# A decoder layer with sparse experts: VectorE instead of GpSimd computes the remainders and the modulation in front of the first expert

## The chip, the cores and the metric

The kernel runs on 1 core of one Trainium2 chip. The metric is the device time of one execution in microseconds (us). The engines are TensorE (PE, with its weight loads as PEld), VectorE (DVE), ScalarE (ACT), GpSimd (POOL) and SyncE (SP), which issues most DMA transfers. Less is better.

## The reference

One layer on 512 tokens of width 1024, in fp32, with two sub-layers:

```
cond = silu(c)
sh_m, sc_m, gt_m, sh_f, sc_f, gt_f = split(cond @ w_ada + b_ada, 6)
h = rms_norm(x, g_pre_mix) * (1 + sc_m) + sh_m
q_a, k_a, v_a, q_b, k_b, v_b, f = h @ w_in
y_a = attention of 8 heads with a cumulative log-forget-gate bias
y_b = block-sparse attention of 8 heads with a relative-position bias
x = x + gt_m * rms_norm(concat(y_a, y_b) @ w_out, g_post_mix)
h = rms_norm(x, g_pre_ffn) * (1 + sc_f) + sh_f
y = sum over the 4 best of 32 experts: gate * (swiglu(h @ w_gate_up[e] + b) @ w_down[e] + b)
x = x + gt_f * rms_norm(y, g_post_ffn)
```

## The kernel before, in words

**Products in two parts.** TensorE multiplies in the type fp32r, which keeps fewer bits than fp32. Each fp32 operand is therefore split: ScalarE copies it into an fp32r tile (the upper part, `hi`), and a subtraction gives the remainder, `lo = raw - hi`, also in fp32r. A product is the sum of hi x hi, hi x lo and lo x hi. The function `split` (L279 to L282) does this for the weights of the first sub-layer; `lo_part` (L1101) does it for the expert weights.

**Opening (0 to about 61 us).** The modulation vectors are `cond @ w_ada`. They are not computed on TensorE as matrix products; instead the eight row blocks of a column slice are multiplied by one value per partition and added up, and TensorE then sums over the partitions with a column of ones. For the two vectors needed first, shift and scale of the mixing sub-layer (SH_M and SC_M), there are four slices (q = 0 to 3) of 256 columns. Of the eight blocks of a slice VectorE does 5 (SC_M) or 6 (SH_M) in `ada_macs` (L360 for the first, L362 for the others) and GpSimd the remaining 3 or 2 in `ada_pool` (L374, L376). `ada_sums` (L383 on) adds the two partial sums on TensorE (L389), finishes scale and shift on VectorE (L396 to L398), and then applies them to two channels k of the transposed x: ScalarE writes the upper part and the full value (L401), and the remainder (L403) is VectorE's for even k and GpSimd's for odd k. Meanwhile `v_split` splits the weights of V, block by block, with the remainder on GpSimd (`G_`), and `v_mm` (L426) multiplies.

**V and projections (61 to about 125 us).** The second V group follows, with the forget gates and the biases between. `mac_step` (L262, L264) computes the other four modulation vectors on VectorE, 512 columns at a time, in steps spread over this stage and the attention. `qk_split` splits the weights of a query or key projection of two heads (eight blocks of 128 columns, so 128x1024), `qk_proj` (L561 to L563) multiplies, `evac_a` and `evac_b` (L575, L584, L587) take the result out of PSUM.

**Attention (125 to about 345 us).** There is one turn per head h, and a turn issues the work of neighbouring heads: a projection, the second product of head h-1, the transposes of head h's weights (`stage_b`, L667 to L671), the scores of head h+1, then its softmax (L631 on VectorE, L634 on ScalarE) and `normalize` (L643, L647: four products of 128, 256, 384 and 512 columns on VectorE). Behind the normalization come the next `qk_split` or, from head 11 on, `wo_split` for the output weights, and two `mac_step`s. `mix_out` (L694 to L701) adds the two halves of a head pair and splits the result for the output product; its remainder (L701) is GpSimd's.

**Output product, norms and router (345 to about 405 us).** Row blocks of 128 tokens pass through `wo_mm`, `post_norm`, `norm_h` and the router (`route_a`, L1003 to L1010). In `norm_h` GpSimd keeps two products and sums of 128x1024 (L971, L972). The raising to a power in `rstd` (L227) is GpSimd's as well. The first weight tile of the first expert is split just before the last `route_a`, with the remainder on GpSimd (L1101).

**Experts (from about 405 us).** Expert 0's rows are gathered from HBM by an indirect DMA that GpSimd issues (L1177); the number of tokens per expert gives the order of the others (`order_rank`, `order`). Its result `perm` (L1426) releases the stream of the other experts' weights, 12 tiles of 1 MB each, that SyncE issues as slots come free. Their remainders are VectorE's already. Only the second and third tile of expert 0 are shared: columns 0 to 1407 (`LO_V`) on VectorE, 1408 to 2047 on GpSimd.

**What sets the order.** The program is written out by hand: each engine runs its instructions in the order in which the code issues them, and waits at the head of its queue for what the next one needs. A weight tile's slot comes free (`W.release`) when its readers are done, and this lets SyncE issue the next load.

Of the kernel before, what the change touches and what calls it, by code (L numbers as in the profile page):

```python
# [11 lines left out]
F32 = mybir.dt.float32  # L12
# [4 lines left out]
OP = mybir.AluOpType  # L17
# [4 lines left out]
RING2, RING3 = 3, 1  # L22
LO_V = 1408

# [72 lines left out]
def build(tc, io, dbg=None):  # L97
    nc = tc.nc
    with ExitStack() as ctx:
# [180 lines left out]
        def split(raw, hi, lo, lo_eng=None):  # L280
            nc.scalar.activation(hi, raw, AF.Copy)  # L281
            (lo_eng or nc.gpsimd).tensor_tensor(lo, raw, hi.bitcast(F32), op=OP.subtract)  # L282

# [12 lines left out]
        with ExitStack() as st:  # L296
# [51 lines left out]

            NPE = {SC_M: 3, SH_M: 2}
            aq, todo_q = {}, [(q, ch, k) for q in range(4) for ch in (SC_M, SH_M) for k in range(8 - NPE[ch])]  # L350

            def ada_macs(n):

                for _ in range(n):
                    q, ch, k = todo_q.pop(0)
                    if k == 0:
                        aq[q, ch] = xp.tile([128, 256], F32, name="accq", tag="accq", bufs=4)
                    a, w, c = aq[q, ch], W.tiles[ada_ids[ch, q]], cond[:, k:k + 1]
                    if k == 0:
                        nc.vector.tensor_scalar(a, w[:, k], c, None, op0=OP.mult)  # L360
                    else:
                        nc.vector.scalar_tensor_tensor(a, w[:, k], c, a, op0=OP.mult, op1=OP.add)  # L362
                    if k == 7 - NPE[ch]:
                        W.release(ada_ids[ch, q])

            def ada_pool(q, ch):
                if not NPE[ch]:
                    return
                w = W.tiles[ada_ids[ch, q]]
                X = [128, 256]  # L370
                ts = xp.tile([128, 2, 256], F32, name="accp", tag="accp", bufs=2)
                for k in range(8 - NPE[ch], 8):
                    t = ts[:, k % 2]
                    nc.gpsimd.tensor_tensor(t, w[:, k], cond[:, k:k + 1].to_broadcast(X), op=OP.mult)  # L374
                    if k > 8 - NPE[ch]:
                        nc.gpsimd.tensor_tensor(t, t, u, op=OP.add)  # L376
                    u = t
                aq[q, ch, 1] = u

            def ada_sums(q):  # L380

                ps = {}
                for ch in (SC_M, SH_M):  # L383
                    a = aq.pop((q, ch))
                    p = ps[ch] = ps1.tile([128, 2], F32, name="adaq", tag="adac", bufs=2)
                    parts = [aq.pop((q, ch, 1)), a] if NPE[ch] else [a]
                    for n, a in enumerate(parts):
                        for j in range(2):
                            nc.tensor.matmul(p[:, j:j + 1], a[:, 128 * j:128 * j + 128], ones,  # L389
                                             start=(n + j == 0), stop=(n + j == len(parts)))  # L390
                if AHEAD_Q[q]:
                    for ch in (SC_M, SH_M):
                        ada_pool(q + 1, ch)
                ada_macs(AHEAD_Q[q])
# [4 lines left out]
                for k in range(2 * q, 2 * q + 2):  # L399
                    for o in (hT[:, 0, k], xT[:, k]):  # L400
                        nc.scalar.activation(o, xT[:, k], AF.Identity, scale=a_m[:, k:k + 1], bias=modT[:, k:k + 1])  # L401
                    eng = nc.gpsimd if k % 2 else nc.vector
                    eng.tensor_tensor(hT[:, 1, k], xT[:, k], hT[:, 0, k].bitcast(F32), op=OP.subtract)  # L403

# [42 lines left out]

            G_ = nc.gpsimd
            per_q = len(todo_q) // 4
            AHEAD_Q = (3, 5, 6, 0)  # L450
            for ch in (SC_M, SH_M):
                ada_pool(0, ch)
            ada_macs(per_q)
# [7 lines left out]
            for q in range(4):  # L461
                if q < 3 and not AHEAD_Q[q]:
                    for ch in (SC_M, SH_M):
                        ada_pool(q + 1, ch)
                if q < 3:
# [84 lines left out]
        with ExitStack() as st:  # L550
# [135 lines left out]
            def mix_out(h):  # L686
# [9 lines left out]
                if s:  # L696
                    if p % 4 == 0:
                        MIX[g] = big.tile([128, 4, 2, 512], F32R, name="mix", tag="big")
                    m = MIX[g]
                    nc.scalar.activation(m[:, p % 4, 0], y, AF.Copy)  # L700
                    nc.gpsimd.tensor_tensor(m[:, p % 4, 1], y, m[:, p % 4, 0].bitcast(F32), op=OP.subtract)  # L701

# [185 lines left out]
        with ExitStack() as st:  # L888
# [218 lines left out]
            first[0] = hi_lo(first_raw(0))  # L1107
            lo_part(nc.gpsimd, first_raw(0), *first[0], 0, 2048)
            W.release(moe_ids[0, 0], False)
# [368 lines left out]
        order_rank()  # L1478
        for n in (1, 2):
            lo_part(nc.vector, first_raw(n), *first[n], 0, LO_V)  # L1480
            lo_part(nc.gpsimd, first_raw(n), *first[n], LO_V, 2048)
            W.release(moe_ids[0, n])
        nc.gpsimd.memset(xg[1], 0.0)
        blocks[0].w = first
        stage_x(blocks[0].tiles[0])
        for i, (p, n) in enumerate(seq[:-LAST]):
# [170 lines left out]
```

## Time and profile before

| | us |
|---|---|
| median of 3 runs | 1579.89 (1579.83 to 1581.43) |
| the profiled execution | 1584.43 |
| span of its profile | 1582.4 |
| busy in the span: TensorE, VectorE, ScalarE, GpSimd | 1431.8, 1004.6, 756.6, 367.8 |
| HBM read | 466.80 MB, 308 GB/s over the span |

The profile shows one execution. Its times are in us from the start of the span, and L12 is line 12 of the kernel. "Busy" is the time in which an engine executes instructions; a matrix product's end is modelled, so a busy TensorE need not be TensorE at its peak. The granted clock (PEclk) is 1.00 at full speed and 0.50 at half. A row names an engine, a line and an operation, then what is written, "<-" and what is read, with the shape; in brackets stands the idle time in front of it and what ended it.

### The profile page before, as it was taken

To read this page: it belongs to the slowest core of one execution; us is meant where nothing else is said; L and a number is where in the kernel's file an instruction comes from. 1 tells how busy PE (TensorE), PEld (TensorE's weight loads), DVE (VectorE), ACT (ScalarE), POOL (GpSimd) and SP (SyncE) were. 2 spreads that over 40 slices of the span, in tenths; PEclk is the share of its full clock that TensorE was granted. 3 is DMA by queue.
4 is the path that set the end of the run, shared out by engine and by line. 5 is a ranking of instruction groups with operands and counts; after the bars stand their busy time and mean duration, and the time that the engine had idled before them with its cause. 6 is when DMAs were issued, how large, how long until landed. Compare 5 with 4: busy or idle time off the path is not lost. (4 is left out here: it accounts for less than half of the span.)

```text
span 1582.4 us, 18315 instructions
## 1 busy us (share of the span) xinstructions
PE 1431.8 (90%) x6513; PEld 952.2 (60%) x6513; DVE 1004.6 (63%) x1287; ACT 756.6 (48%) x833; POOL 367.8 (23%) x268
## 2 busy tenths in 40 slices
PE   5898999989599999889999989998999999999992
PEld 4676777667475655647575646646565746666640
DVE  6785888876876664837374655727374748686532
ACT  5433565545364462726263553616263646475421
POOL 7542234434310212310010203310001203121002
PEclk8897999789699999999999999998999999999996
DMA  9652353364498999999699999999699999999994
GB/s 304 219 192 89 93 173 100 105 224 181 164 353 286 385 398 374 397 395 383 246 392 355 384 401 386 399 390 375 205 390 344 394 381 400 388 381 388 357 393 119
DMA packets 154757, 485.92 MB, mean 307 GB/s; under 512 B 13775, under 2 KB 35387, under 8 KB 154664
## 3 DMA queue, kind: packets, MB, share of 16 engines
q1 hardware_dynamic: 143807, 457.39, 76.8%
q0 software_dynamic: 10016, 24.59, 6.6%
q10 hardware_dynamic: 841, 2.75, 0.5%
q8 instruction: 52, 0.85, 0.2%
q14 instruction: 41, 0.34, 0.1%
HBM read 466.80 MB, written 19.85 MB: 308 GB/s over the span
## 5 line engine op out<-in xcount | busy, mean ns | idle before, releaser
L1101 DVE TENSOR_TENSOR mlo<-raw,mhi 128x2048 fp32r<-128x2048 f32 (+1 forms) x203 | 457.9, 2279 | 140.2 <-ACT mhi L1097 139.9
L1097 ACT ACTIVATE mhi<-raw 128x2048 fp32r<-128x2048 f32 x203 | 385.8, 1912 | 152.4 <-PE gu L1217 59.6
L1217 PE MATMUL gu<-mhi,xT 128*128 128x512 f32 x1152 | 402.0, 417 | 0.6 <-DVE xT L1193 0.6
L1322 POOL DMA_INDIRECT accd<-y,idx x33 | 116.8, 3539 | 811.9 <-ACT y L1320 749.7
L1217 PEld LDWEIGHTS gu<-mhi,xT 128*128 128x128 f32 x1152 | 221.3, 192 | 54.0 <-issue 3.4
L1217 PE MATMUL gu<-mlo,xT 128*128 128x512 f32 x608 | 243.9, 401 | 1.1 <-DVE mlo L1101 1.1
L1231 PE MATMUL gu<-raw,xT 128*64 128x512 f32 x960 | 234.0, 597 | 1.1 <-DMA raw<-in_w_gate_up 0.9
L1217 PE MATMUL gu<-mhi,aT 128*128 128x512 f32 x576 | 205.4, 427 | 6.1 <-ACT mhi L1097 6.1
L1231 PEld LDWEIGHTS gu<-raw,xT 128*64 128x64 f32 x960 | 82.6, 136 | 103.9 <-issue 90.2
L1217 PEld LDWEIGHTS gu<-mhi,aT 128*128 128x128 f32 x576 | 114.0, 198 | 42.0 <-ACT mhi L1097 10.5
L1217 PE MATMUL gu<-mlo,aT 128*128 128x512 f32 x304 | 125.0, 411 | 9.3 <-DVE mlo L1101 9.3
L1217 PEld LDWEIGHTS gu<-mlo,xT 128*128 128x128 f32 x608 | 116.7, 192 | 27.6 <-DVE mlo L1101 2.9
L1231 PE MATMUL gu<-raw,aT 128*64 128x512 f32 x480 | 118.1, 616 | 5.7 <-ACTq L1515 3.5
L282 POOL TENSOR_TENSOR wlo<-raw,whi 128x1024 fp32r<-128x1024 f32 (+1 forms) x35 | 71.1, 2043 | 107.1 <-ACT whi L281 90.6
L1177 POOL DMA_INDIRECT xg<-h2d,idx x32 | 60.8, 1899 | 113.4 <-issue 70.4
L1281 PE MATMUL gu<-bt,selb 96*64 96x512 bf16 (+1 forms) x204 | 81.6, 400 | 0.0
L1290 ACT ACTIVATE y<-gu 64x1024 f32<-64x1024 f32 x16 | 16.3, 1021 | 133.4 <-PE gu L1231 131.9
L1231 PEld LDWEIGHTS gu<-raw,aT 128*64 128x64 f32 x480 | 40.4, 140 | 65.9 <-issue 57.2
L1306 DVE TENSOR_SCALAR li<-gu 128x1024 f32<-128x1024 f32 x17 | 20.8, 1223 | 92.1 <-PE gu L1217 84.9
L1217 PEld LDWEIGHTS gu<-mlo,aT 128*128 128x128 f32 x304 | 59.9, 197 | 25.2 <-DVE mlo L1101 12.0
L561 PE MATMUL pq<-hT,whi 128*128 128x512 f32 x128 | 57.5, 450 | 6.6 <-DVE qs L584 6.6
L1292 DVE TENSOR_TENSOR y<-gu,y 64x1024 f32<-64x1024 f32 x16 | 19.5, 1216 | 68.7 <-ACT y L1290 68.7
(335 smaller groups left out, 1884.4 us busy)
## 6 DMA issues: line engine op xcount, KB each, us to landing
raw<-in_w_gate_up SPq DMA_DIRECT2D x255, 1024.0 KB, 16.6
raw<-in_w_down SPq DMA_DIRECT2D x128, 1024.0 KB, 16.8
raw<-in_w_ada SPq DMA_DIRECT2D x20, 1024.0 KB, 8.1
raw<-in_w_in SPq DMA_DIRECT2D x12, 1024.0 KB, 7.7
rawx<-in_w_ada SPq DMA_DIRECT2D x4, 1024.0 KB
raw<-in_w_out SPq DMA_DIRECT2D x4, 1024.0 KB, 5.0
accd<-zeros SPq DMA_DIRECT2D x5, 512.0 KB
x_sb<-in_x SPq DMA_DIRECT2D x4, 512.0 KB
```

What stands on the lines that cost most here:

```text
L282: (lo_eng or nc.gpsimd).tensor_tensor(lo, raw, hi.bitcast(F32), op=OP.subtract)
L561: nc.tensor.matmul(ps, hi[:, k], hT[:, 0, k], start=(k == 0), stop=False)
L1097: nc.scalar.activation(hi, raw, AF.Copy)
L1101: eng.tensor_tensor(lo[:, a:b], raw[:, a:b], hi[:, a:b].bitcast(F32), op=OP.subtract)
L1177: nc.gpsimd.indirect_dma_start(out=T.x[:T.m], out_offset=None, in_=h2d, in_offset=bass.IndirectOffsetOnAxis(ap=T.idx[:T.m, :1], axis=0), b ...
L1217: nc.tensor.matmul(ps, x, w, start=start and i == 0, stop=stop and i == len(p) - 1)
L1231: nc.tensor.matmul(ps[a:a + 64], self.t[:, kt], w, start=kt < 2, stop=kt > 5)
L1281: nc.tensor.matmul(ps[:T.n], sel, bt[:, o:o + 512], start=False, stop=False)
L1290: nc.scalar.activation(t, T.ps[q][T.n:2 * T.n], AF.Copy)
L1292: nc.vector.tensor_tensor(t, T.ps.pop(q)[:T.n], t, op=OP.add)
L1306: nc.vector.tensor_scalar(t, v, -6.0, 8.0, op0=OP.max, op1=OP.min)
L1322: nc.gpsimd.indirect_dma_start(out=accd, out_offset=idx, in_=T.y[:T.m], in_offset=None, bounds_check=S + 127, oob_is_err=True, compute_op= ...
```

## The change

All remainders in front of the first expert are computed on VectorE, and VectorE does the whole of the first modulation.

- `split` takes VectorE as its default engine, `G_` for V's weights is VectorE, the remainder of `mix_out` and that of all channels k in `ada_sums` are VectorE's.
- `ada_pool` is gone; `ada_macs` does all eight blocks, and `ada_sums` adds only VectorE's sums (two TensorE products a vector instead of four).
- The first expert weight tile's remainder is VectorE's at the same place in the code. The second and third tile's are whole on VectorE; the transposes of expert 0's rows (`stage_x`) are issued between them instead of behind both, and the clearing of the second row buffer comes ahead of both.

GpSimd keeps the power in `rstd`, `norm_h`'s L971 and L972, a copy of keys (L588), the clearing of buffers and its DMA issues.

```diff
         def split(raw, hi, lo, lo_eng=None):
             nc.scalar.activation(hi, raw, AF.Copy)
-            (lo_eng or nc.gpsimd).tensor_tensor(lo, raw, hi.bitcast(F32), op=OP.subtract)
+            (lo_eng or nc.vector).tensor_tensor(lo, raw, hi.bitcast(F32), op=OP.subtract)
...
-            NPE = {SC_M: 3, SH_M: 2}
-            aq, todo_q = {}, [(q, ch, k) for q in range(4) for ch in (SC_M, SH_M) for k in range(8 - NPE[ch])]
+            aq, todo_q = {}, [(q, ch, k) for q in range(4) for ch in (SC_M, SH_M) for k in range(8)]
...
-                    if k == 7 - NPE[ch]:
+                    if k == 7:
                         W.release(ada_ids[ch, q])
-
-            def ada_pool(q, ch):
...
-                    parts = [aq.pop((q, ch, 1)), a] if NPE[ch] else [a]
-                    for n, a in enumerate(parts):
-                        for j in range(2):
-                            nc.tensor.matmul(p[:, j:j + 1], a[:, 128 * j:128 * j + 128], ones,
-                                             start=(n + j == 0), stop=(n + j == len(parts)))
-                if AHEAD_Q[q]:
-                    for ch in (SC_M, SH_M):
-                        ada_pool(q + 1, ch)
+                    for j in range(2):
+                        nc.tensor.matmul(p[:, j:j + 1], a[:, 128 * j:128 * j + 128], ones, start=j == 0, stop=j == 1)
                 ada_macs(AHEAD_Q[q])
...
-                    eng = nc.gpsimd if k % 2 else nc.vector
-                    eng.tensor_tensor(hT[:, 1, k], xT[:, k], hT[:, 0, k].bitcast(F32), op=OP.subtract)
+                    nc.vector.tensor_tensor(hT[:, 1, k], xT[:, k], hT[:, 0, k].bitcast(F32), op=OP.subtract)
...
-            G_ = nc.gpsimd
+            G_ = nc.vector
...
-                    nc.gpsimd.tensor_tensor(m[:, p % 4, 1], y, m[:, p % 4, 0].bitcast(F32), op=OP.subtract)
+                    nc.vector.tensor_tensor(m[:, p % 4, 1], y, m[:, p % 4, 0].bitcast(F32), op=OP.subtract)
...
-            lo_part(nc.gpsimd, first_raw(0), *first[0], 0, 2048)
+            lo_part(nc.vector, first_raw(0), *first[0], 0, 2048)
...
         order_rank()
-        for n in (1, 2):
-            lo_part(nc.vector, first_raw(n), *first[n], 0, LO_V)
-            lo_part(nc.gpsimd, first_raw(n), *first[n], LO_V, 2048)
-            W.release(moe_ids[0, n])
         nc.gpsimd.memset(xg[1], 0.0)
         blocks[0].w = first
-        stage_x(blocks[0].tiles[0])
+        for n in (1, 2):
+            lo_part(nc.vector, first_raw(n), *first[n], 0, 2048)
+            W.release(moe_ids[0, n])
+            if n == 1:
+                stage_x(blocks[0].tiles[0])
```

## Rows read from the trace of the kernel before

**Rows 1.** Busy time by stage: us, busy of each engine (instructions), granted clock, DMA.

```profile
0.00:61.00 61.00, 36.30 (x158) 29.14 (x159) 43.51 (x78) 28.29 (x42) 42.84 (x57) 0.81 0.95 305
61.00:125.00 64.00, 55.66 (x235) 40.32 (x236) 53.81 (x64) 26.17 (x40) 25.98 (x16) 0.93 0.54 175
125.00:296.00 171.00, 165.87 (x754) 126.37 (x753) 134.09 (x284) 90.17 (x208) 52.84 (x41) 0.92 0.36 112
296.00:345.00 49.00, 39.52 (x136) 29.32 (x136) 40.09 (x92) 21.42 (x47) 23.13 (x48) 0.69 0.41 133
...
419.00:1582.00 1163.00, 1075.99 (x4942) 679.01 (x4940) 679.77 (x639) 556.96 (x432) 194.51 (x85) 0.97 0.97 360
```

**Rows 2.** Opening, VectorE's L362 (first) and L360 alone: us, busy (instructions).

```profile
0.00:61.00 61.00, 31.55 (x36) 0.81 0.95 305
...
0.00:61.00 61.00, 5.40 (x8) 0.81 0.95 305
```

**Rows 3.** VectorE's instructions in order of time: start, us, line, operation.

```profile
41.44 0.35 DVE L360 TENSOR_SCALAR accq<-rawx,cond 128x256 f32<-128x256 f32 x1
41.82 1.00 DVE L362 SCALAR_TENSOR_TENSOR accq<-rawx,cond,accq 128x256 f32<-128x256 f32 x2
...
73.77 3.11 DVE L264 SCALAR_TENSOR_TENSOR acc<-rawx,cond,acc 128x512 f32<-128x512 f32 x4
...
114.63 0.48 DVE L262 TENSOR_SCALAR acc<-raw,cond 128x512 f32<-128x512 f32 x1
...
137.49 1.27 DVE L647 TENSOR_SCALAR P<-P,st 128x128 f32<-128x128 f32 x4
```

**Rows 4.** VectorE's subtractions by shape: busy, mean ns, idle in front and its releaser.

```profile
L403 DVE TENSOR_TENSOR hT<-xT,hT 128x512 fp32r<-128x512 f32 x3 | 2.1, 708 | 5.2 <-ACT xT L401 5.2
...
L446 DVE TENSOR_TENSOR bw<-bw,bp 96x1024 f32<-96x1024 f32 x2 | 2.4, 1219 | 1.1 <-ACT bp L442 1.1
...
L1101 DVE TENSOR_TENSOR mlo<-raw,mhi 128x2048 fp32r<-128x2048 f32 x2 | 4.6, 2292 | 1.5 <-ACT mhi L1097 1.5
```

**Rows 5.** 61 to 133 us: VectorE's groups, TensorE's wait, three windows (columns: rows 1).

```profile
L264 DVE SCALAR_TENSOR_TENSOR acc<-raw,cond,acc 128x512 f32<-128x512 f32 x21 | 25.9, 1232 | 0.7
...
L262 DVE TENSOR_SCALAR acc<-raw,cond 128x512 f32<-128x512 f32 x3 | 3.3, 1108 | 0.0
...
124.60 0.77 PE L561 MATMUL pq<-hT,whi 128*128 128x512 f32 x1 [6.56 <-DVE qs L584]
...
104.40:110.00 5.60, 5.60 (x26) 4.50 (x25) 5.46 (x5) 2.48 (x5) 3.07 (x2) 1.00 0.31 97
124.60:132.70 8.10, 8.10 (x24) 6.49 (x25) 1.26 (x2) 0.00 (x0) 0.00 (x0) 0.67 0.73 252
85.70:124.50 38.80, 30.65 (x137) 22.90 (x135) 37.78 (x42) 15.03 (x21) 18.13 (x10) 0.94 0.63 205
```

**Rows 6.** Attention: VectorE's L647 alone (as rows 2), and a wait of TensorE.

```profile
125.00:296.00 171.00, 33.83 (x52) 0.92 0.36 112
...
PE pt L667 <- DVE P L647: 3.5, 5, 1.3
```

**Rows 7.** Tail of the attention: L647 alone, L264 alone, and a wait of TensorE.

```profile
296.00:345.00 49.00, 14.70 (x12) 0.69 0.41 133
...
296.00:345.00 49.00, 7.27 (x7) 0.69 0.41 133
...
PE pt L667 <- DVE P L647: 4.1, 3, 2.0
```

**Rows 8.** Hand-over: two comparisons, GpSimd's remainder, its gathers (ns, shortest/median/longest).

```profile
393.21 0.29 DVE L1007 TENSOR_TENSOR oh<-iotaf,i 128x128 f32<-128x128 f32 x1
...
397.26 3.69 DVE L1007 TENSOR_TENSOR oh<-iotaf,i 128x128 f32<-128x128 f32 x1
...
395.46 5.34 POOL L1101 TENSOR_TENSOR mlo<-rawt,mhi 128x2048 fp32r<-128x2048 f32 x1 [1.44 <-ACT mhi L1097]
...
L1177 POOL DMA_INDIRECT xg<-h2d,idx x2: 1136/1768/2399, 404.6 to 431.6; - x2
```

More of the change, by code (lines that the diff above doesn't have):

```diff
@@ L22 @@
 RING2, RING3 = 3, 1
-LO_V = 1408
 CAP = [128, 128, 64, 128, 64, 120, 60, 104, 60, 192, 56, 100, 56, 96, 52, 92, 48, 88, 44, 160, 40, 84, 40, 84, 36, 80, 76, 36, 72, 68, 32, 28]
@@ L362, in ada_macs @@
                         nc.vector.scalar_tensor_tensor(a, w[:, k], c, a, op0=OP.mult, op1=OP.add)
-                    if k == 7 - NPE[ch]:
+                    if k == 7:
                         W.release(ada_ids[ch, q])
-            def ada_pool(q, ch):
[L367 to L378, printed above, removed]
             def ada_sums(q):
@@ L446, in bias_part @@
                     nc.vector.tensor_tensor(bw, bw, bp, op=OP.subtract)
-            G_ = nc.gpsimd
+            G_ = nc.vector
             per_q = len(todo_q) // 4
             AHEAD_Q = (3, 5, 6, 0)
-            for ch in (SC_M, SH_M):
-                ada_pool(0, ch)
             ada_macs(per_q)
@@ L461, in build @@
             for q in range(4):
-                if q < 3 and not AHEAD_Q[q]:
-                    for ch in (SC_M, SH_M):
-                        ada_pool(q + 1, ch)
                 if q < 3:
```

## The prediction

> **What bounds the kernel now.** I read the stage table first [rows 1]. From 419 us on, the experts' weights stream: the DMA engines are busy 97% of the time at 360 GB/s. That stage can begin only when the order of the experts is known, and its length does not depend on VectorE's or GpSimd's earlier work. So whatever the change does to the time before 419 us moves the end by the same amount, one to one. Before 419 us TensorE leads in places and waits in others: it is busy 36 of 61 us in the opening, 56 of 64 in the next stage, 166 of 171 in the attention, and only 39.5 of 49 us in the attention's tail, where its granted clock averages 0.69. VectorE is 71 to 84% busy in these stages.
>
> The second thing to see is that VectorE's own instructions there are stretched. In the opening, 36 multiply-adds take 31.55 us and 8 products 5.40 us [rows 2]: 0.88 and 0.68 us each. Where GpSimd computes nothing alongside, the same forms take 0.50 and 0.35 us, the 512-wide multiply-add 3.11/4 = 0.78 us, its opening product 0.48 us, and the four normalizing products of a head 1.27 us together [rows 3]. The stretched ones lie beside a GpSimd operation on SBUF, as the comparison of 128x128 at 397 us does [rows 8]. So the work to be moved costs VectorE time already, without being in its queue. The argument is a ledger: what VectorE gets back against what it must add.
>
> **The change, step by step.** What a moved instruction costs on VectorE is read from rows of the same shape [rows 4]: 0.70 us for 128x512 in SBUF, 1.22 us for 1024 columns, 2.29 us for 2048. No queue is passed by a moved transfer; the DMA issues that GpSimd keeps come sooner in its queue, if anything. The sixteen small products on TensorE that summed GpSimd's halves are dropped; I count them at nothing, because TensorE waits for VectorE's accumulators there.
>
> *Opening.* Back: 31.55 + 5.40 - 36 x 0.50 - 8 x 0.35 = 16.1 us. Added: 20 multiply-adds x 0.50 = 10.0; eight V remainders x 0.70 = 5.6; three odd-channel remainders x 0.70 = 2.1. These three also make VectorE stand still until ScalarE's later output; I take 0.9 us each, half of what the even channels wait now (5.2/3 = 1.7 us), so 2.6. Together +20.3 - 16.1 = +4.2 us. The last two V remainders (1.4 us) stand behind the accumulators that TensorE waits for. So **TensorE gets the last sums 2.8 us later**, and the V products behind them move with it. The ends: 0 if the standing still is covered, +6 if each of these waits is the full 1.7 us and the two remainders count.
>
> *V and the first projection.* From 85.7 to 124.5 us VectorE is busy 37.78 of 38.80 us, and TensorE waits 6.56 us for the last of that queue [rows 5]. Back: 25.9 - 21 x 0.78 = 9.5 and 3.3 - 3 x 0.48 = 1.9. Added: four V remainders, 2.8, and three of the projection, 3.7. Net -4.9 us. With the late start, TensorE resumes at 124.6 + 2.8 - 4.9, that is 2.1 us earlier, after a wait of 1.7 us in place of 6.56. The 24 products behind the present wait took 8.1 us at a granted clock of 0.67; the 24 before it took 5.6 us at 1.00 [rows 5]. I take the short wait to leave the clock up: another -2.5. **Sum to the first scores: -4.6 us.** The ends: +2 (late by 6, the clock falling all the same) and -7.4 (no late start).
>
> *Attention.* Normalizing gives back 33.83 - 13 x 1.27 = 17.3 us; 13 remainders x 1.22 and five of the mix x 0.70 add 19.4. VectorE's load goes from 134 to 136 of 171 us, with the multiply-adds' gain left out, so TensorE's stream stays the bound. TensorE's waits for the normalized scores are 3.5 us [rows 6]. The new remainders stand behind the normalization in the queue, which itself ends sooner; so I take -2.5. The ends are 0 and -3.5, and above it what a standing queue costs (a rival below).
>
> *Tail of the attention.* Here the output weights are split while TensorE waits. Back: 14.70 - 3 x 1.27 = 10.9 and 7.27 - 7 x 0.78 = 1.8. Added: seven remainders x 1.22 and three x 0.70 = 10.6. The load shrinks by only 2.1 us, but the order counts: the normalization that TensorE waits 4.1 us for [rows 7] comes ahead of the remainders. I take -4.5, the 4.1 and a little of the other idle time. The ends: -2.1, and -9.5, all of TensorE's idle time there (49.0 - 39.5).
>
> *Hand-over to the experts.* One comparison of 128x128 that takes 0.29 us at 393 us lasts 3.69 us at 397 us, beside GpSimd's remainder of the first weights, which runs from 395.46 to 400.8 us [rows 8]: 3.4 back. That remainder is now issued ahead of it on VectorE: 2.29 added. Behind it stand the router's choice, the token positions and the gather of the first expert's rows. The gather took 1.14 us on GpSimd, a later one beside VectorE's remainder of 2048 columns 2.40 us [rows 8]; VectorE now starts its next remainder close behind the gather's issue, so I add 0.3 between the ends 0 and 1.3. Net **-0.8 us**. The two further remainders grow by 0.7 us each and lie beside TensorE's first expert products; if that cover is gone they cost 1.4 us. The page "SBUF — State Buffer", in its box on the "DVE blocks DMA" trap, of the Trainium skill speaks against this step: a gather issued from GpSimd cannot write its descriptors while VectorE holds the shared port pair. The trace's 2.40 against 1.14 us agrees with it; by the rule at its hardest the gather waits out a whole remainder of 2.29 us, and the sum below would be 2 us less, still inside the forecast's case.
>
> **Sum:** -4.6 - 2.5 - 4.5 - 0.8 = -12.4 us. The profiled execution took 1584.43 us (span 1582.4 and 2.0 around it), so it would take 1572.0. It lies 4.5 us above the median of the runs, 1579.89, so the forecast for the median is **1567.5 us**.
>
> **Rivals.** *More: the clock.* In the tail TensorE computes 39.5 us at a mean grant of 0.69. If shorter waits bring that to 1.00, up to 39.5 x 0.31 = 12 us more go; half of it gives 1561.5. For it: the products at 0.67 right behind the long wait [rows 5]. Against it: the small score products of the tail stay.
>
> *Less: given back.* VectorE becomes the pacer of the opening (late by 6 us, not 2.8), the attention gives nothing and the tail only its 2.1 us: -4.6 + 3.2 = -1.4, then -2.1 and -0.8, about -4.3: 1575.6. For it: VectorE is the one that TensorE and ScalarE wait for in the opening, and it gets more to do. If the clock falls behind the 1.7 us wait too, the 2.5 goes and -1.8 is left, 1578: no change.
>
> *Slower: a standing queue.* Each remainder waits at the head of VectorE's queue for ScalarE's upper half, and everything behind it (the softmax of the next head) waits along. GpSimd could stand there free of charge. VectorE has 171 - 136 = 35 us to spare over 13 heads, 2.7 us a head; beyond that each further us costs 13. To end 0.2% slower it must stand 2.7 + (12.4 + 3.2)/13 = 3.9 us a head; at 4.5 us the time is 1567.5 + 13 x 1.8 = 1591. Against it: the upper half is issued on ScalarE right behind the exponentials, and VectorE's normalization lies between.
>
> *It doesn't do what it says.* If the stretch is not GpSimd's doing, VectorE keeps its long instructions and adds 20.3 + 6.5 + 10.6 us in the opening, the second stage and the tail: some 1617. Against it: the same forms at 0.50 and 0.88 us in one stage.
>
> **How the numbers follow.** The forecast (a gain of 8 to 16 us) has 0.56, more by the clock 0.15, given back 0.16, no change 0.06, slower 0.07 (0.05 standing queue, 0.02 no release). 0.2% is 3.2 us, about what a measurement of this kernel can tell from no change. So faster 0.87, same 0.06, slower 0.07. The range 1557 to 1577 takes in the forecast with its bounds, the bigger gain and most of the smaller one; what it leaves out is no change, slower and the ends of the clock's case, less than 2 in 10.
>
> **What would show it.** Right: normalizing falls from 48.5 us (both stages) towards 16 x 1.27 = 20; the opening's multiply-adds are 0.50 us each though there are 56; the wait of 6.56 us is 1 to 3 us; the expert order comes 10 to 16 us before 419, and the stage behind it keeps its 1163 us. Wrong: multiply-adds that stay at 0.8 us or more, TensorE's wait at the opening's last sums longer by over 6 us, new waits of TensorE on the softmax in mid-attention, or an expert stage whose length moves by more than 3 us.

## The result and the profile after it

The median went from 1580.66 us (4 runs, 1579.83 to 1582.95) to **1552.86 us** (4 runs, 1548.54 to 1553.57): 27.8 us less, ratio 0.9821 with a 95% interval of 0.9803 to 0.9838. The same kernel once more, on another chip (below), took 1554.08 against 1580.85: 26.8 us less. The forecast was 12.4 us less, and the fast end of the range was 1557: too small a gain.

Three profiles are read in this section. The profiled execution of before took 1584.43 us, 3.8 above the median beside it; the changed kernel's first took 1548.54, its lowest run and 4.3 below its median; its second took 1557.45, 3.4 above its median. The first pair therefore shows 35.9 us, the second 27.0, which is what the medians say. I read sizes from the second pair and name the first where it differs; the views below the tables are of the changed kernel's first profile.

The stage table, with the columns of [rows 1], is cut at the same events in each: the last sums of the modulation, the first product of the fourth group of 24 projection products, the last projection product, the last router row's transposes, and the expert order. Before:

```profile
0.00:61.10 61.10, 36.40 (x158) 29.24 (x159) 43.60 (x78) 28.29 (x42) 42.84 (x57) 0.81 0.95 304
61.10:137.60 76.50, 68.16 (x286) 49.84 (x286) 56.77 (x74) 28.96 (x49) 25.98 (x16) 0.90 0.53 173
137.60:290.50 152.90, 147.77 (x671) 112.59 (x672) 126.62 (x267) 83.76 (x193) 51.43 (x39) 0.92 0.34 104
290.50:341.30 50.80, 41.32 (x158) 30.58 (x157) 42.38 (x71) 25.04 (x53) 21.55 (x13) 0.73 0.41 135
341.30:417.90 76.60, 61.04 (x300) 50.08 (x301) 55.35 (x160) 32.49 (x66) 31.52 (x59) 0.80 0.47 171
417.90:1582.40 1164.50, 1077.09 (x4946) 679.88 (x4945) 679.92 (x640) 558.06 (x432) 194.51 (x85) 0.97 0.97 359
```

The changed kernel, first profile:

```profile
0.00:61.20 61.20, 34.55 (x126) 26.68 (x127) 42.39 (x109) 28.28 (x42) 4.12 (x14) 0.82 0.96 304
61.20:128.70 67.50, 65.30 (x286) 47.79 (x284) 51.37 (x86) 28.64 (x49) 2.30 (x3) 0.96 0.60 195
128.70:268.10 139.40, 138.53 (x672) 106.90 (x672) 117.76 (x285) 83.73 (x194) 12.43 (x21) 0.99 0.37 116
268.10:313.70 45.60, 35.31 (x158) 26.53 (x157) 38.44 (x82) 24.93 (x53) 2.48 (x3) 0.83 0.45 145
313.70:388.70 75.00, 61.18 (x301) 50.55 (x302) 51.85 (x161) 32.71 (x66) 22.27 (x55) 0.81 0.48 175
388.70:1546.70 1158.00, 1069.67 (x4945) 676.57 (x4944) 679.85 (x640) 557.56 (x432) 191.75 (x85) 0.97 0.97 361
```

and its second profile:

```profile
0.00:61.50 61.50, 35.55 (x126) 27.59 (x127) 42.28 (x109) 28.30 (x42) 4.14 (x14) 0.82 0.95 303
61.50:130.30 68.80, 66.62 (x286) 48.97 (x285) 52.23 (x90) 29.57 (x50) 2.29 (x3) 0.95 0.59 192
130.30:274.60 144.30, 143.53 (x671) 110.54 (x672) 119.06 (x284) 82.85 (x192) 12.47 (x21) 0.95 0.36 112
274.60:320.00 45.40, 36.91 (x159) 27.14 (x157) 36.22 (x79) 24.96 (x53) 1.77 (x3) 0.85 0.45 152
320.00:394.00 74.00, 60.33 (x303) 49.95 (x304) 51.76 (x161) 33.10 (x66) 22.29 (x55) 0.82 0.48 173
394.00:1555.60 1161.60, 1073.89 (x4944) 677.67 (x4942) 679.64 (x641) 557.22 (x432) 196.10 (x85) 0.97 0.97 360
```

| stage | forecast | second profile | first profile |
|---|---|---|---|
| opening | +2.8 | +0.4 | +0.1 |
| V and the first projection | -7.4 | -7.7 | -9.0 |
| attention | -2.5 | **-8.6** | **-13.5** |
| tail of the attention | -4.5 | -5.4 | -5.2 |
| hand-over to the experts | -0.8 | -2.6 | -1.6 |
| experts | 0 | -2.9 | -6.5 |
| sum | -12.4 | -26.8 | -35.7 |

The first thing to see is the attention, the third row of each table. The products are the same (671 or 672), yet TensorE is busy 147.77 us before and 143.53 or 138.53 after, at a granted clock of 0.92 against 0.95 or 0.99; and its idle time (length less busy) falls from 5.1 to 0.8 or 0.9 us. The second is the experts' row: that stage is 1164.5 us in before's profile and between 1156.2 and 1162.4 in all the others of this study. The longest but one is experiment 6's, which is built on the kernel before, but the two shortest (1156.2 both) are from the slow kernels of experiments 4 and 8, so there is no order that follows the time ahead of the stage. I take its 2.9 and 6.5 as variation between executions; no run tests it.

VectorE's instructions became as short as forecast. The opening's multiply-adds and first products alone, then the normalizing products of attention and tail (the views of [rows 2, 6, 7]):

```profile
0.00:61.00 61.00, 27.14 (x56) 0.82 0.96 305
...
0.00:61.00 61.00, 2.80 (x8) 0.82 0.96 305
...
125.00:268.00 143.00, 16.57 (x52) 0.99 0.37 116
268.00:316.00 48.00, 3.83 (x12) 0.81 0.47 153
```

56 multiply-adds at 0.485 us where 36 had taken 0.88 each; normalizing 20.4 us, where 48.5 was and 20 was forecast. TensorE's waits in the first profile, grouped (in total, times, longest), from 61 to 130 us and then in the attention:

```profile
PE pb L568 <- ACT bias L569: 1.7, 1, 1.7
PE pq L533 <- DVE qs L556: 0.5, 1, 0.5
...
PE pcs L785 <- DVE tl L643: 0.6, 1, 0.6
PE prw L715 <- DVE tl L643: 0.2, 1, 0.2
```

The 6.56 us for VectorE [rows 5] are 0.5; ScalarE's bias, 1.7 us before as well, is now what is late there. The wait for normalized scores (3.5 us, [rows 6]) has no row left in the attention. In the tail the 4.1 us of [rows 7] are gone too, but another wait has grown in their place, that for the remainders of the transposed scores. The first line is of the kernel before, the others of the changed one:

```profile
PE pt L667 <- DVE tl L671: 1.8, 1, 1.8
...
PE pt L639 <- DVE tl L643: 5.2, 3, 2.4
PE pS L589 <- DVE st L603: 2.2, 1, 2.2
```

So TensorE's idle time in the tail hardly changes: 9.5 us before, 10.3 and 8.5 in the changed kernel's two profiles. What fell there is its busy time.

### The profile page after: what moved, and what is told of

Same layout as the page of the kernel before. It is cut to its first block, busy times and chain, and to the rows that moved or that the text cites. A ratio compares the mean times of both kernels' runs of the same rounds, so it can differ in the third digit from the quotient of the medians.

```text
span 1546.7 us, 18202 instructions
## 1 busy us (share of the span) xinstructions
PE 1404.5 (91%) x6481; PEld 935.0 (60%) x6481; DVE 981.7 (63%) x1360; ACT 755.9 (49%) x833; POOL 235.4 (15%) x181
## 5 line engine op out<-in xcount | busy, mean ns | idle before, releaser
L1073 DVE TENSOR_TENSOR mlo<-raw,mhi 128x2048 fp32r<-128x2048 f32 x203 | 459.2, 2285 | 137.7 <-ACT mhi L1069 137.4
L1203 PE MATMUL gu<-raw,aT 128*64 128x512 f32 x480 | 114.9, 602 | 5.8 <-ACTq L1487 3.5
L1163 ACT ACTIVATE xT<-ptr 128x512 fp32r<-128x512 f32 (+1 forms) x51 | 28.7, 596 | 70.0 <-PE ptr L1162 69.8
L1165 DVE TENSOR_TENSOR aT<-ptr,aT 128x512 fp32r<-128x512 f32 x36 | 23.2, 685 | 60.9 <-ACT aT L1163 60.9
## 6 DMA issues: line engine op xcount, KB each, us to landing
rawx<-in_w_ada SPq DMA_DIRECT2D x4, 1024.0 KB, 12.1
```

The source lines that it names most:

```text
L1073: eng.tensor_tensor(lo[:, a:b], raw[:, a:b], hi[:, a:b].bitcast(F32), op=OP.subtract)
L1163: nc.scalar.activation(hi, pt, AF.Copy)
L1165: nc.vector.tensor_tensor(lo, pt, hi.bitcast(F32), op=OP.subtract)
L1203: nc.tensor.matmul(ps[a:a + 64], self.t[:, kt], w, start=kt < 2, stop=kt > 5)
```

## The experiments

Each run has runs of the kernel before beside it on the same chip. Experiments 1 to 4 ran on one chip (before: 1581.68), 5 to 7 and the changed kernel once more on another (before: 1580.85), 8 on a third (before: 1579.52). Behind each median stand in brackets its ratio to the kernel before on the same chip and the ratio's 95% interval.

**1. The attention's remainders back on GpSimd.** Everything else stays as changed.

```diff
-            split(raw, hi, lo)
+            split(raw, hi, lo, nc.gpsimd)
...
-                    nc.vector.tensor_tensor(m[:, p % 4, 1], y, m[:, p % 4, 0].bitcast(F32), op=OP.subtract)
+                    nc.gpsimd.tensor_tensor(m[:, p % 4, 1], y, m[:, p % 4, 0].bitcast(F32), op=OP.subtract)
...
-                split(W.tiles[wo_ids[k // 2]][:, k % 2], hi, lo)
+                split(W.tiles[wo_ids[k // 2]][:, k % 2], hi, lo, nc.gpsimd)
```

> The changed kernel with the remainders of the projections, of the output weights and of the mix back on GpSimd; everything else stays VectorE's. Theory (GpSimd's subtractions stretch VectorE's instructions, TensorE waits for these, and its clock falls behind the waits): normalizing goes from 20.4 us back to over 40 us, the granted clock of the attention from 0.99 to about 0.92, and most of the gain is lost: 1568 to 1576 us. Rival (the attention gains because it starts in better order out of the earlier stages): the clock stays above 0.97 and the time below 1560.

1573.92 us (ratio 0.9954, 0.9937 to 0.9970): of the 27.8 us, 7.8 are left. So about 20 us hang on these three edits, which the forecast had put at 2.5 + 4.5 and a part of the first projection's. Stage table of its attention, VectorE's normalizing group there (as in [rows 4]) and TensorE's wait for it:

```profile
134.70:285.70 151.00, 144.11 (x671) 109.20 (x672) 126.19 (x267) 84.07 (x193) 50.91 (x39) 0.96 0.34 105
...
L619 DVE TENSOR_SCALAR P<-P,st 128x128 f32<-128x128 f32 (+3 forms) x52 | 33.8, 715 | 0.5
...
PE pt L639 <- DVE P L619: 5.2, 7, 2.2
```

Normalizing is back at the 33.8 us of [rows 6], and TensorE is idle for 6.9 us of the attention again. The clock is not back: it was expected at about 0.92 and is 0.96, and TensorE's busy time, 144.11 us, is near the 143.53 of the changed kernel's second profile.

**2. The opening as before** (GpSimd's products, the odd channels, V's remainders), all later remainders on VectorE.

```diff
-            aq, todo_q = {}, [(q, ch, k) for q in range(4) for ch in (SC_M, SH_M) for k in range(8)]
+            NPE = {SC_M: 3, SH_M: 2}
+            aq, todo_q = {}, [(q, ch, k) for q in range(4) for ch in (SC_M, SH_M) for k in range(8 - NPE[ch])]
...
-                    nc.vector.tensor_tensor(hT[:, 1, k], xT[:, k], hT[:, 0, k].bitcast(F32), op=OP.subtract)
+                    eng = nc.gpsimd if k % 2 else nc.vector
+                    eng.tensor_tensor(hT[:, 1, k], xT[:, k], hT[:, 0, k].bitcast(F32), op=OP.subtract)
...
-            G_ = nc.vector
+            G_ = nc.gpsimd
```

> The changed kernel with the opening as before (GpSimd's share of the modulation, of the odd channels and of V's remainders); the attention and the hand-over stay VectorE's. Theory: only the second stage's share comes back, 2 to 6 us, since the opening itself ended at the same time in both kernels: 1555 to 1559 us, and the attention's clock stays above 0.97. Rival (the earlier stages set the attention's clock): clock about 0.92 and 1565 us or more.

1556.14 us (0.9834, 0.9814 to 0.9853). **3. The hand-over as before:**

```diff
-            lo_part(nc.vector, first_raw(0), *first[0], 0, 2048)
+            lo_part(nc.gpsimd, first_raw(0), *first[0], 0, 2048)
...
-            lo_part(nc.vector, first_raw(n), *first[n], 0, 2048)
+            lo_part(nc.vector, first_raw(n), *first[n], 0, LO_V)
+            lo_part(nc.gpsimd, first_raw(n), *first[n], LO_V, 2048)
```

> The changed kernel with the three remainders of the first expert's tiles and the order around them as before. Theory: from the end of the tail to the expert order 75.0 us become 76.6 us, the time 1553 to 1556 us. Rival (the stretched comparison was covered): no difference to the changed kernel, within 0.5 us from the tail to the order.

1554.13 us (0.9825, 0.9801 to 0.9848). Against the before of their own chip they keep 25.5 and 27.6 us of the 27.8, and both intervals overlap that of the whole change: neither the opening's 2 us nor the hand-over is clear of noise in the medians. In the profiles the opening as before ends at 61.0 us but the attention begins at 132.9, 2.6 to 4.2 us later than in the changed kernel, and the attention itself takes 142.1 us at a clock of 0.97; so GpSimd's work in the opening is not what had held the attention up. The hand-over as before takes 76.4 us, 1.4 to 2.4 more than in the changed kernel's two profiles.

**4. The sharing alone.** VectorE does all that it does in the changed kernel; GpSimd repeats the remainders of the projection and output weights beside it, in quarters, into a scratch tile that nothing reads.

```diff
+        shadow = long1.tile([128, 256], BF, name="shadow")
+
+        def beside(raw, hi):
+            out = shadow if len(raw.shape) == 2 else shadow.rearrange("p (k c) -> p k c", k=2)
+            nc.gpsimd.tensor_tensor(out, raw, hi.bitcast(F32), op=OP.subtract)
...
+            for k in range(0, 8, 2):
+                beside(raw[:, k:k + 2], hi[:, k:k + 2])
...
+                for c in range(0, 1024, 256):
+                    beside(W.tiles[wo_ids[k // 2]][:, k % 2, c:c + 256], hi[:, c:c + 256])
```

> The changed kernel, and beside each remainder of a projection or an output weight GpSimd subtracts the same operands once more, in four pieces of 256 columns, into a scratch tile that nothing reads. VectorE's own work is that of the changed kernel. Theory (sharing, not load): the multiply-adds and the normalizing products stretch again, to 0.9 us and over 25 us, the attention's clock falls to 0.94 or less and the time is 1563 to 1580 us. Rival (GpSimd cost time because its results came late, two times slower): nothing waits for the scratch tile, so the time stays at 1553 us.

1576.18 us (0.9971, 0.9956 to 0.9985): against the kernel before, 5.5 us are left of the change's 26.8 to 27.8, so work whose result nobody uses costs 21 to 22 us. The attention and the tail of this run, and VectorE's normalizing and multiply-adds in the attention:

```profile
136.60:291.50 154.90, 149.43 (x671) 114.39 (x672) 133.20 (x282) 83.31 (x192) 69.42 (x72) 0.91 0.33 102
291.50:345.90 54.40, 38.64 (x158) 29.02 (x157) 46.60 (x82) 24.97 (x53) 33.32 (x33) 0.78 0.40 131
...
L627 DVE TENSOR_SCALAR P<-P,st 128x384 f32<-128x384 f32 (+3 forms) x50 | 19.5, 454 | 0.4
...
L263 DVE SCALAR_TENSOR_TENSOR acc<-raw,cond,acc 128x512 f32<-128x512 f32 x19 | 21.9, 1154 | 0.4
```

VectorE's busy time grows from 119.06 to 133.20 us with the same instructions, the 512-wide multiply-add from 0.75 to 1.15 us; TensorE's idle time goes to 5.5 us and its clock to 0.91. The dose is not that of the kernel before: GpSimd is busy 69.4 us there (51.4 before), and more of the stretch lies in the multiply-adds, less in the normalizing (454 ns a product, 715 in experiment 1). GpSimd's reading can also keep a weight tile's slot: eight loads are issued up to 4.5 us later for it, 21.2 us in sum, but no wait of TensorE, VectorE or ScalarE for a weight tile or for GpSimd's scratch tile is in the trace from 104 us to the end of the tail. Where no shadow work was added (opening, hand-over) the stages take 61.5 and 74.4 us, as in the changed kernel. So the price was GpSimd's work beside VectorE's, whoever computes the remainder that is used.

**5. GpSimd works, but reads nothing.** As in 4, with eight fills in place of four subtractions.

```diff
+        def beside(raw, hi):
+            nc.gpsimd.memset(shadow, 0.0)
+            nc.gpsimd.memset(shadow, 0.0)
```

> The changed kernel, and beside every remainder of the projection weights and of the output weights GpSimd fills a scratch tile with zeros (8 fills of 128x256, which read nothing). Nothing waits for the fills; what is computed is unchanged. If it is GpSimd's reading of SBUF that stretches VectorE's instructions, the normalizing products stay near 24 us in sum (52.6 in the kernel before, 24.4 in the changed one) and the multiply-adds near 0.5 us each, and the time stays at 1550 to 1557 us. If any work of GpSimd on SBUF stretches them, the normalizing products go back to 30 to 50 us in sum, and the time to 1562 to 1577 us.

1556.03 us (0.9847, 0.9827 to 0.9867), as the changed kernel beside it. The same two groups of VectorE, and one of the two of GpSimd's fills:

```profile
L627 DVE TENSOR_SCALAR P<-P,st 128x512 f32<-128x512 f32 (+3 forms) x49 | 17.4, 428 | 0.4
...
L263 DVE SCALAR_TENSOR_TENSOR acc<-raw,cond,acc 128x512 f32<-128x512 f32 x19 | 14.2, 749 | 0.4
...
L286 POOL MEMSET shadow<- 128x256 bf16 x48 | 16.6, 345 | 2.2
```

With 32 us of fills beside it the multiply-add keeps its 749 ns, and the normalizing product goes from some 383 to 428 ns. (The 0.5 us of the expectation is the 256-wide form's.) In time the fills are near what GpSimd did there in the kernel before: 51.4 us of work in the attention against 12.4 in the changed kernel, so 39 us, beside which the two took 960 and 715 ns. But a fill is short, 0.33 us, where a remainder took some 2.5. The Trainium skill, "SBUF — State Buffer", section "Who interferes with whom", says that an instruction of VectorE with two inputs in SBUF meets GpSimd only where GpSimd reads SBUF, and that its two-port forms, `tensor_scalar` among them, meet any of GpSimd's. Both halves agree with these two rows; that fills as long as a remainder would stretch as little is not shown.

**6. Does TensorE's clock fall because of its short waits?** The kernel before, with three products in front of the first transposes of twelve heads, where TensorE waits for normalized scores.

```diff
+                    if h < 12 and part == 0:
+                        for _ in range(3):
+                            nc.tensor.matmul(pt, hT[:, 0, 0, 0:128], hT[:, 0, 0], start=True, stop=True)
```

> The kernel before, with three products of 128x512 more (into a PSUM tile that is overwritten behind them) ahead of the first transposes of each of the first 12 heads: 36 products of some 0.21 us, 7.7 us of TensorE's work that the result does not need. If attention in the kernel before is long because the granted clock falls behind TensorE's short waits, the fillers stand in those waits, the granted clock of attention goes from 0.92 to 0.97 or more, and the time is no longer than before, 1574 to 1582 us. If the clock falls for another reason, it stays near 0.92 and the time rises by the fillers, to 1584 to 1590 us.

1584.81 us (1.0025, 1.0014 to 1.0036): at the second theory's edge, with a clock between the two.

```profile
137.90:294.80 156.90, 154.12 (x707) 117.79 (x708) 126.56 (x267) 83.66 (x193) 51.39 (x39) 0.94 0.33 101
```

36 such products are 8.4 us at the pace of [rows 5] (24 in 5.6 us); 2.4 us of them went into idle time (5.1 to 2.8), and the other products' busy time fell by about 2 (154.12 - 8.4 = 145.7 against 147.77). Covering half of the idle time thus brought back about half of the distance from 147.77 to the changed kernel's second profile (143.53), but a fifth of that to the first (138.53). One profile can't tell the two apart: that the short waits set the clock is neither borne out nor excluded.

**7. VectorE's waits in the opening, filled.** The changed kernel, with five of the next slice's multiply-adds moved into the waits for ScalarE's even and odd channels, behind each of the first three slices: fifteen in all.

```diff
                 for k in range(2 * q, 2 * q + 2):
                     for o in (hT[:, 0, k], xT[:, k]):
                         nc.scalar.activation(o, xT[:, k], AF.Identity, scale=a_m[:, k:k + 1], bias=modT[:, k:k + 1])
+                    if q < 3:
+                        ada_macs((3, 2)[k % 2])
...
-                    ada_macs(per_q - AHEAD_Q[q])
+                    ada_macs(per_q - AHEAD_Q[q] - 5)
```

> The changed kernel, with five of the next slice's multiply-adds of the opening issued in VectorE's waits for ScalarE (three behind the even channels of a block, two behind the odd ones) and not all behind the block. The work is the same, only VectorE's order in the opening differs. If VectorE's waits of 0.8 to 0.9 us for ScalarE's outputs are what is left of slack in the opening, the opening ends 3 to 6 us sooner and the time is 1546 to 1551 us. If the opening is set by the loads or by ScalarE, it ends within 1 us of where it did, and the time is that of the changed kernel beside it.

**1546.84 us** (5 runs, 1542.43 to 1549.33; 0.9784, 0.9765 to 0.9804): faster than both kernels. The remainders of the modulated channels in the opening, in the changed kernel and here, with VectorE's idle time in front of them behind the bar:

```profile
L380 DVE TENSOR_TENSOR hT<-xT,hT 128x512 fp32r<-128x512 f32 x6 | 4.2, 692 | 7.8 <-ACT xT L379 7.8
```

```profile
L382 DVE TENSOR_TENSOR hT<-xT,hT 128x512 fp32r<-128x512 f32 x6 | 4.2, 693 | 1.3 <-ACT xT L379 1.2
...
0.00:55.00 55.00, 33.87 (x128) 26.82 (x129) 41.84 (x109) 28.30 (x42) 4.02 (x14) 0.90 0.99 315
```

7.8 us of standing still became 1.3, and the opening ends at 55.0 us in place of 61.2 to 61.5. The DMA share there is 0.99, against 0.95 or 0.96, so the loads can't come much closer together. VectorE itself waits 0.7 us for a load in this profile, and TensorE still 8.0 us for VectorE's accumulators.

> The changed kernel itself, on the same chip as the three others, to compare them with. By the runs so far 1549 to 1554 us; if its profiled run was not a lucky one, the expert order ends 387 to 390 us from the start of the span.

The changed kernel beside them took 1554.08 us (5 runs, 1549.72 to 1557.45; 0.9831, 0.9814 to 0.9849); its stages are the third table above, and its expert order comes at 394, not at 387 to 390: the first profile was a quick one.

**8. VectorE's time without any sharing.** The changed kernel, each normalizing product followed by one of the same size that multiplies by 1.0.

```diff
                     nc.vector.tensor_scalar(P[:, o:o + n], P[:, o:o + n], st_[:, 2, i:i + 1], None, op0=OP.mult)
+                    nc.vector.tensor_scalar(P[:, o:o + n], P[:, o:o + n], 1.0, None, op0=OP.mult)
```

> The changed kernel, with each normalizing product followed by a second one of the same size that multiplies by 1.0: the result is the same, VectorE's normalizing goes from 24.5 us back to some 49 us in sum, as long as it is in the kernel before, and nothing is shared, as GpSimd does no more than in the changed kernel. If the sharing cost its time through VectorE alone (the products stand in front of TensorE's transposes), TensorE idles 3 to 7 us in attention again (5.1 in the kernel before, 0.8 in the changed one), attention takes 149 to 154 us and not 139 to 144, and the time is 1563 to 1574 us. If VectorE's time there is hidden and the sharing cost TensorE its time in another way, attention stays at 139 to 146 us and the time at 1552 to 1559 us.

1570.34 us (0.9941, 0.9923 to 0.9959). The attention, VectorE's two groups there and TensorE's waits:

```profile
130.30:289.10 158.80, 152.02 (x671) 114.30 (x672) 135.63 (x337) 83.60 (x193) 12.43 (x21) 0.91 0.33 102
...
L619 DVE TENSOR_SCALAR P<-P,st 128x128 f32<-128x128 f32 (+3 forms) x52 | 19.9, 383 | 0.5
L620 DVE TENSOR_SCALAR P<-P 128x128 f32<-128x128 f32 (+3 forms) x52 | 17.0, 328 | 1.8
...
PE pt L640 <- DVE P L620: 3.7, 7, 1.4
PE pb L568 <- DVE yp L668: 2.1, 3, 0.9
```

GpSimd does no more than in the changed kernel, yet the attention takes 158.8 us, more than the 149 to 154 of the first theory: TensorE idles 6.8 us, as expected, but its busy time for the same products grows as well, from 143.53 to 152.02, at a granted clock of 0.91. So VectorE's time alone is enough to bring back the idle time, the low clock and the long attention, and 17 us of work on an engine that is busy 119 of 144 us cost 14.5. The dose is somewhat more than the sharing's (VectorE is busy 135.6 us, 126.6 in the kernel before); that the sharing has no second way to TensorE is not shown, only that none is needed.

## Why the prediction was wrong

**Opening: the sign of the cost held, the size was 2.4 us or more off.** The stage ends 0.1 to 0.4 us later, not the 2.8 that were taken from +4.2 for VectorE's queue. The forecast added 0.70 us for each subtraction; two of them in a row, in VectorE's order of time, take 1.29 us together:

```profile
33.17 1.29 DVE L281 TENSOR_TENSOR wlo<-raw,whi 128x512 fp32r<-128x512 f32 x2
```

So the second begins 0.60 behind the first, and a queue of them is shorter than the sum of their durations. That is a small part: the eight V remainders came to 5.2 us where the ledger had 5.6, and the multiply-adds with their first products to 29.9 where it had 30.8. The rest is in terms that it left out: VectorE's smaller instructions shrank as well (the four additions L397 from 1.5 to 0.6 us), and its other waits are about 1 us shorter. In all its busy time fell by 1.2 to 1.3 us, where the ledger without the waits has +1.6. The waits for ScalarE were sized right (1.7 us for an even channel and 0.9 for an odd one, 1.3 on average, and the six in the opening stand 7.8), and experiment 7 shows that they were slack.

**V and the first projection: right.** -7.7 against -7.4. TensorE's wait for VectorE shrank a little more than forecast (to 0.5 us, not 1.7, as the opening was not late), and the 24 products behind it went at the full clock, as forecast:

```profile
119.20:125.00 5.80, 5.76 (x25) 4.62 (x25) 2.53 (x3) 2.41 (x3) 0.00 (x0) 1.00 1.07 378
```

5.8 us where [rows 5] has 8.1 at 0.67.

**Attention: this is the step that failed**, "TensorE's stream stays the bound ... so I take -2.5. The ends are 0 and -3.5". The direction was the right one (normalized scores come sooner, and TensorE's waits for them go), but two things failed. The ledger let VectorE's load go "from 134 to 136", "with the multiply-adds' gain left out". In the stages of the tables above it went from 126.6 to 119.1 us: the added remainders cost 19.3 us as forecast and normalizing gave back 17.7, but the multiply-adds and their first products gave back 7.9 more. Before, then the second profile:

```profile
L264 DVE SCALAR_TENSOR_TENSOR acc<-raw,cond,acc 128x512 f32<-128x512 f32 x20 | 19.2, 960 | 0.4
L262 DVE TENSOR_SCALAR acc<-raw,cond 128x512 f32<-128x512 f32 x3 | 5.8, 1920 | 0.0
...
L263 DVE SCALAR_TENSOR_TENSOR acc<-raw,cond,acc 128x512 f32<-128x512 f32 x21 | 15.7, 749 | 0.4
L261 DVE TENSOR_SCALAR acc<-raw,cond 128x512 f32<-128x512 f32 x3 | 1.4, 481 | 0.0
```

And the term and its ends were sized from one row of waits, 3.5 us, with TensorE's 148 us of busy time taken as fixed. All of TensorE's idle time there was 5.1 us, and 4.3 of it went. And the busy time is not fixed: the same products took 4.2 us less in the second profile and 9.2 in the first. The stage measured -8.6 and -13.5. "TensorE's stream stays the bound" is what the runs contradict. In the eleven profiles the length of the attention follows VectorE's busy time about one for one, though TensorE is busy 95 to 99% of it (us; experiment 6 holds 8.4 us of fillers):

| kernel | VectorE busy | length | TensorE busy | TensorE idle | clock |
|---|---|---|---|---|---|
| changed, first profile | 117.8 | 139.4 | 138.5 | 0.9 | 0.99 |
| experiment 5 | 118.6 | 141.3 | 140.4 | 0.9 | 0.97 |
| changed, second profile | 119.1 | 144.3 | 143.5 | 0.8 | 0.95 |
| experiment 2 | 119.6 | 142.1 | 141.2 | 0.9 | 0.97 |
| experiment 7 | 119.6 | 142.2 | 141.3 | 0.9 | 0.97 |
| experiment 3 | 119.8 | 140.7 | 139.8 | 0.9 | 0.98 |
| experiment 1 | 126.2 | 151.0 | 144.1 | 6.9 | 0.96 |
| experiment 6 | 126.6 | 156.9 | 154.1 | 2.8 | 0.94 |
| before | 126.6 | 152.9 | 147.8 | 5.1 | 0.92 |
| experiment 4 | 133.2 | 154.9 | 149.4 | 5.5 | 0.91 |
| experiment 8 | 135.6 | 158.8 | 152.0 | 6.8 | 0.91 |

Experiment 8 shows it from the other side (VectorE's time, without sharing, brings the idle time and the low clock back), experiment 4 that the sharing does it, experiment 1 that these remainders carry some 20 of the 27.8 us together with those of the tail. The forecast did price the clock, but behind the one long wait and, as a rival, in the tail, not where TensorE computes longest.

What sets the clock inside the attention is left open, and with it how much of the 4.2 us of busy time is the change's: experiment 1 has 6.9 us of idle time and a busy time of 144.1, next to the second profile's. Over the eleven profiles, those with under 1 us of idle time there stand at 0.95 to 0.99, those with 2.8 us or more at 0.91 to 0.96. The Trainium skill, "TensorE: Matmul & The Clock Gate", section "A second HAM failure mode: psum-queue depth-cycling", says that short idle times between groups of products can keep the clock moving between its two levels, 1.2 and 2.4 GHz; the split of the eleven profiles agrees, experiment 6 agrees in its sign only, and the changed kernel's two profiles differ by 5.0 us of busy time (143.53 and 138.53) with the same idle time.

**Tail: the number by luck, not by its reason.** -5.4 against -4.5. The -4.5 was to be the wait of 4.1 us and a little of the other idle time. That wait went, but the wait for the transposed remainders grew from 1.8 to 4.5 us (5.2 in the first profile), and TensorE's idle time fell by 1.0 us only (in the first profile it rose by 0.8). What came in its place is busy time, 4.4 us less (41.32 to 36.91, clock 0.73 to 0.85; 6.0 less in the first profile): a part of what the first rival had put here, up to 12 us by the clock.

**Hand-over: right in sign, -2.6 (-1.6 in the first profile) against -0.8.** The comparison of 3.69 us [rows 8] is 0.29 again, behind a remainder of 2.28:

```profile
369.45 2.28 DVE L1073 TENSOR_TENSOR mlo<-rawt,mhi 128x2048 fp32r<-128x2048 f32 x1
...
372.45 0.29 DVE L979 TENSOR_TENSOR oh<-iotaf,i 128x128 f32<-128x128 f32 x1
...
376.40 1.15 POOL L1149 DMA_INDIRECT xg<-h2d,idx  x1 [9.28 <-DVE less L1388]
...
376.88 2.27 DVE L1073 TENSOR_TENSOR mlo<-raw,mhi 128x2048 fp32r<-128x2048 f32 x1
```

The 0.3 us for the gather was not needed: it starts 0.48 us ahead of VectorE's next remainder and takes 1.15 us. From the gather's issue to the expert order it is 13.3 us before and 12.1 to 12.3 after, a gain for which the ledger had nothing. The order of the two is what counts: of the 31 gathers in the expert stage of the first profile, the 16 that start while a remainder runs on VectorE take 1.89 to 4.79 us, the other 15 take 0.99 to 1.22. The box of the Trainium skill, "SBUF — State Buffer", that the prediction weighed there speaks of VectorE's two-port operations, and by the same page `tensor_tensor`, a remainder's operation, has no two-port mode. These gathers do wait beside it, so here the measurement says more than that box; at the hand-over the gather came first.

**The rivals.** That it doesn't do what it says fell with the 0.485 us of the multiply-adds. Given back fell with the opening's +0.4. The standing queue fell too: in the changed kernel's attention VectorE is idle 0.0 us in front of its 13 remainders:

```profile
L281 DVE TENSOR_TENSOR wlo<-raw,whi 128x1024 fp32r<-128x1024 f32 x13 | 15.8, 1217 | 0.0
```

**The sum of the miss.** Of the 14.4 us between forecast and second pair the attention has 6.1, the experts 2.9, the opening 2.4, the hand-over 1.8, the tail 0.9 and the second stage 0.3. The experts' 2.9 no experiment ties to the change. The prediction gave a move of more than 3 us there as a sign of being wrong, and the first pair has 6.5; but from profile to profile this stage moves by some 8 us, and a forecast that is set against one profile inherits that.

## What to carry to other kernels

Where TensorE is "97% busy" at a mean granted clock of 0.92, its busy time is no floor: the same products took 138.5 to 143.5 us in the profiles where it waited under 1 us and 144.1 or more in the others, so let the range of such a stage reach down to its busy time at full clock, and not only by its listed waits, and look at the engine that it waits for: the attention's length followed VectorE's busy time, with VectorE busy some 83% of it. Before work is given to GpSimd because it idles, look whether VectorE's instructions get longer beside it; here 21 to 22 us of the end hung on that, and work that reads nothing (short fills) cost nothing that the runs can tell. And an engine that takes over work should get it in the places where it stands still: fifteen multiply-adds moved into VectorE's waits gave another 7 us.

## What was not expected of the hardware

Work of VectorE can cost TensorE more than the idle time that it makes: in experiment 8, 6.0 us more of idle time came with 8.5 us more of busy time for the same 671 products. In experiment 1 nearly the same idle time (6.9 us) came with 0.6 us of it only (144.11 against 143.53), so one profile does not price the clock. And VectorE's products by a constant are shorter than those by a column (328 against 383 ns in experiment 8, same shapes); no run tests whether the constant or the place behind the other product makes it.
